# Sums of squares of q in a gated DeltaNet layer: block turns, row sums and one 0/1 product in place of eight one-column products

## The chip, the cores and the metric

The kernel runs on one core of a Trainium2 chip. The metric is device time in microseconds (us) of that core; the time of a kernel is the median of several executions. Five engines matter here: TensorE (PE in the profile; its weight loads are shown apart as PEld), VectorE (DVE), ScalarE (ACT), GpSimd (POOL) and SyncE (SP), which here only starts transfers.

## The reference

One decoder layer on 256 tokens of width 2048, all in float32. Cut to what matters:

```python
h = rmsnorm(x, norm_mix_w)
proj = h @ w_in                       # q, k, v, z, b, a, p_in, g_a, g_b
q, k, v = split(silu(causal_dwconv([q, k, v], conv_qkv_w)))
q = l2norm(q.reshape(1, 256, 16, 128)) * 128 ** -0.5   # per token and head
k = l2norm(k.reshape(1, 256, 16, 128))
o = gated_delta_rule(q, k, v, g_log, beta)   # chunks; a triangular solve in each
o = rmsnorm(o, gdn_norm_w) * silu(z)
mixed = sigmoid(g_a) * o + sigmoid(g_b) * pool_mixer(p_in)
x = x + mixed @ w_out
x = x + (gelu(causal_dwconv(gate)) * up) @ w_down   # gate, up = rmsnorm(x) @ w_up
y = rmsnorm(x, norm_final_w)
```

`l2norm` divides by the root of the sum of squares over the 128 dimensions of a head. A row of `o` is linear in its row of `q`, and `o` goes through an RMS norm, so the kernel doesn't normalise q at all: the sum of squares of q only enters the epsilon term of that norm. It needs one such sum for every token and head: 256 tokens by 4 heads in each of four groups of heads.

## The kernel before, in words

**Weights.** All weights stream from memory in tiles of 256 x 512 float32 (half a MB), in the order in which they are used. `weights()` (L102) hands out the next tile and starts the preparation of the tile two further on: SyncE loads it to `raw` (L112), ScalarE makes a rounded copy `whi` (L121), VectorE the rest `wlo = raw - whi` (L128). `whi` and `wlo` have three buffers each, so the copy for a tile can start once PE is through with the tile three places ahead of it.

**Products.** `gemm_a` (L147) multiplies the 256 tokens by 512 columns of weights: for each tile 4 times three products of 128 x 128 by 512 columns (L158 high by high, L159 low by high, L160 high by low), accumulated in a PSUM tile `psm`. After each half of a tile it calls `side()` (L134), which advances a generator by one `yield`: this is how the small work of the token mixer is written into the stream of large products.

**The loop over groups.** `for g in range(4)` (L779) handles four heads: projections k, q, v, then the pooling mixer, z and the gate, each a `gemm_a` over 8 tiles. After k and q their convolution and SiLU (`conv_silu`, L555) leave `kq` [128 dimensions, 4 heads, k or q, 256 tokens]. Then the generator `gdn` (L575) becomes the side work. In its order:

- decays `dec0`, `dec1` and Gram products k·k and k·q (L620, L622), scaled into `ga0`, `ga1` on DVE (L635, L639); the diagonals of k·k give the sums of squares of k (L625)
- the diagonal 32 x 32 blocks go to memory and come back spread over the partitions as `lb` (L653, L656)
- 31 steps of forward substitution on DVE (L665, L667) that read `lb` and write `tb`; `tb` goes to memory and comes back as blocks of `TTa` (L672, L675)
- four block turns `Ta <- TTa` on DVE (L686), then small products that complete the inverse (L699, L709, L719, L727) and apply it (L734, L739, L744; `w1`, `w2` are copied by ScalarE, L735 and L745)
- the outputs `po` (L752, L754, L755); the squares of q in place (L749, ScalarE); the sums of squares of q, `pn` (L760); squares of `po` on ScalarE and their sums on DVE (L765, L766); `ro` from both (L768, L769), a power on POOL (L770), the scaled output `on` (L772, L775).

`gated()` (L838) finishes the generator and multiplies `on` by the gates (L840, L841); `mixed()` turns the result (L203) for the output projection. After the fourth group eight tiles of the output projection that don't need it are multiplied first (L864).

`lb` and `on` share one buffer with `dec0` (tag "dec0", one buffer): each waits until the one before has been read.

**The order of the work.** Source order isn't engine order. Outside the first stage (`manual_schedule`, L288) the framework's planner orders the instructions of each engine by what its own model finds ready, with source order as priority. Each engine then runs its list strictly in that order and waits on semaphores. In the profile the squares of q (L749) start at 116.5 us in the first group, while the output products beside which they stand in the source (L752) start at 220.3 us.

A float32 product is shown as two MATMULs, each with a weight load of its own. The eight products of L760 in a group are 16 records; the loaded operand is 128 x 128 of squared q, the streamed one a single column of ones:

```python
pn = pg([P, 2, 4])
for t in range(2):
    for h in range(4):
        mm(pn[:, t, h : h + 1], q2[:, h, t * P : (t + 1) * P], ones[:, 0:1], start=True, stop=True)
```

Of the kernel before, what the change touches and what calls it, by code (L numbers as in the profile page):

```python
# [7 lines left out]
F32 = mybir.dt.float32  # L8
F32R = mybir.dt.float32r
I32 = mybir.dt.int32  # L10
AF = mybir.ActivationFunctionType
ALU = mybir.AluOpType

P = 128
S = 256
# [5 lines left out]
EPS = 1e-6  # L21
# [8 lines left out]
WAIT = 5  # L30
# [3 lines left out]
def kernel(  # L34
# [20 lines left out]
    nc = tc.nc  # L55
    mm = nc.tensor.matmul
# [10 lines left out]
    def nm(s):  # L67
        cnt[0] += 1
        return f"{s}_{cnt[0]}"

    def pg(shape=(P, 512)):
        return psg.tile(list(shape), F32, tag="g", name=nm("psg"))
# [135 lines left out]
    ones = cpool.tile([P, P], F32, name="ones")  # L208
    nc.gpsimd.memset(ones, 1.0)
    ident = cpool.tile([P, P], F32, name="ident")  # L210
# [19 lines left out]
    mp = mix.__enter__()  # L230
# [160 lines left out]
    for cq in range(4):  # L391
        pr = slice(32 * cq, 32 * cq + 32)
# [17 lines left out]
    nc.vector.tensor_tensor(id2, ident[:64, 0:32], ident[:64, 32:64], op=ALU.add)  # L410


    pba = pg([P, 2, S])
    for c in range(2):
        hi, lo = weights()
# [59 lines left out]
    for g, win in enumerate(WINDOWS):  # L475
# [3 lines left out]
        for cs in (slice(0, P + PAD), slice(P + PAD, NB)):  # L479
            b = bd[:, cs]  # L480
# [94 lines left out]
    def gdn(g, kq, vt, conv, res):  # L575
# [6 lines left out]
        dec0 = mp.tile([P, 4, S], F32, tag="dec0", name=nm("dec0"))  # L582
# [31 lines left out]
        for hp in range(2):  # L614
# [3 lines left out]
            for h in (h0, h0 + 1):  # L618
# [5 lines left out]
                for t, src in ((0, pg0[:, 0:P]), (1, pg1[:, 0, :])):  # L624
                    nc.vector.tensor_tensor_reduce(jk, src, ident, scale=1.0, scalar=0.0, op0=ALU.mult,  # L625
                                                   op1=ALU.add, accum_out=ssk[:, t, h : h + 1])
# [6 lines left out]
            for h in (h0, h0 + 1):  # L633
# [4 lines left out]
                                               op0=ALU.mult, op1=ALU.mult)  # L638
# [3 lines left out]
                                               op0=ALU.mult, op1=ALU.mult)  # L642
# [12 lines left out]
        for cq in range(4):  # L655
            nc.sync.dma_start(lb[32 * cq : 32 * cq + 32], cdd.rearrange("q (r j) i -> (q r) j i", j=B0))  # L656
        yield
        for _ in range(WAIT):
            yield
        tb = mp.tile([P, 8, B0], F32, tag="tb", name=nm("tb"))  # L660
# [18 lines left out]
        for h in range(4):  # L679
            for t in range(2):  # L680
                nc.scalar.activation(vt[:, t, h, :], vt[:, t, h, :], AF.Copy, scale=nk[:, t, h : h + 1])
        for _ in range(WAIT - 3):
            yield
        for r in range(NR):
            rs = slice(B0 * r, B0 * (r + 1))
            nc.vector.transpose(Ta[rs, :, rs], TTa[rs, :, rs])  # L686
# [50 lines left out]
        pr = pg([P, 4, P])  # L737
# [6 lines left out]
            mm(pw[:, h, :], TT[h // 2][:, 1, h % 2, :], vt[:, 1, h, :], start=True, stop=True)  # L744
        nc.scalar.copy(w2, pw)  # L745
        yield

        q2 = kq[:, :, 1, :]
        nc.scalar.activation(q2, q2, AF.Square)  # L749
        po = [pg([P, 4, P]) for t in range(2)]  # L750
        for h in range(4):
            mm(po[0][:, h, :], ga0[:, h, 256:384], w1[:, h, :], start=True, stop=True)  # L752
# [1 line left out]
            mm(po[1][:, h, :], ga0[:, h, 384:512], w1[:, h, :], start=True, stop=False)  # L754
            mm(po[1][:, h, :], ga1[:, h, P : 2 * P], w2[:, h, :], start=False, stop=True)  # L755
        yield
        pn = pg([P, 2, 4])
        for t in range(2):
            for h in range(4):
                mm(pn[:, t, h : h + 1], q2[:, h, t * P : (t + 1) * P], ones[:, 0:1], start=True, stop=True)  # L760
        ro = mp.tile([P, 2, 4], F32, tag="ro", name=nm("ro"))
        so = mp.tile([P, 2, 4], F32, tag="so", name=nm("so"))
        for t in range(2):
# [1 line left out]
            nc.scalar.activation(o2, po[t], AF.Square, scale=float(P) ** -0.5)  # L765
            nc.vector.tensor_reduce(so[:, t, :], o2, axis=mybir.AxisListType.X, op=ALU.add)  # L766
        yield
        nc.vector.tensor_scalar(ro, pn, EPS * P, EPS * EPS * P, op0=ALU.mult, op1=ALU.add)  # L768
        nc.vector.tensor_tensor(ro, ro, so, op=ALU.add)  # L769
        nc.gpsimd.tensor_tensor(ro, ro, epsx[:, 0:1].unsqueeze(2).to_broadcast([P, 2, 4]), op=ALU.pow)  # L770
        for t in range(2):
# [7 lines left out]
    for g in range(4):  # L779
        kq = mp.tile([P, 4, 2, S], F32, tag="kq", bufs=1, name=nm("kq"))  # L780
# [6 lines left out]
        vt2 = vt.rearrange("p t h d -> p t (h d)")  # L787
        res = []
        later.append(lambda g=g, kq=kq, vt=vt, res=res: side_work.__setitem__(0, gdn(g, kq, vt, v_conv(g, vt), res)))
        v_taps(g)  # L790
        e = evict(gemm_a(xh, xl, KD), rsh)
# [84 lines left out]
    for c in range(4):  # L876
# [9 lines left out]
        for k2 in range(2):  # L886
# [5 lines left out]
            for kk in range(2):  # L892
# [4 lines left out]
                                               op0=ALU.mult, op1=ALU.subtract)  # L897
# [59 lines left out]
    for t in range(2):  # L957
# [14 lines left out]
        for c in (0, 2, 1, 3):  # L972
            xs = xt[:, t, c * 512 : (c + 1) * 512]
            if c < 2:
                nc.vector.scalar_tensor_tensor(xs, xs, rs, nfin[:, c * 512 : (c + 1) * 512],
                                               op0=ALU.mult, op1=ALU.mult)
# [34 lines left out]
```

## Time and profile before

| | |
|---|---|
| median of 3 runs | 1581.47 us (1581.29 to 1581.65) |
| profiled execution | 1581.2 us, span 1579.4 us, mean granted TensorE clock 0.998 |
| busy | PE 1565.1 us, DVE 1066.2 us, ACT 745.4 us, POOL 45.0 us |
| read from memory | 297.56 MB |

The span runs from the first to the last instruction; the 1.8 us by which the profiled execution is longer lie around it. A row of a timeline gives start, length, engine, line, operation, output <- inputs, and in square brackets how long the engine stood idle before the row and what ended that. A row of the chain of waits gives start, length and what ran then on the chain that ended last. A row of groups gives the line, the operation, shapes and count, then busy time and the mean of one, then idle time before. A row of waits gives who waited for whom: us in total, times, the longest.

### The profile page before, as it was taken

The numbers are of one execution on the slowest core, as the hardware profiler recorded it, in microseconds if no ns is written. First come the engines' busy times: TensorE is split into PE (matmuls) and PEld (weight loads), VectorE is DVE, ScalarE is ACT, GpSimd is POOL, SyncE is SP. The second block draws the span as 40 slices with busy tenths as digits, with TensorE's granted clock in tenths as the row PEclk, the third lists the DMA queues.
The fourth block names the chain that finished last, engine by engine and source line by source line (L and its number), as shares of the span: only waits on it lengthen the run. The fifth ranks groups of instructions, "written<-read, shape, count | busy, mean of one in ns | idle before, by whom it ended". The sixth has DMA issues, their size and how long they took to land.

```text
span 1579.4 us, 21330 instructions
## 1 busy us (share of the span) xinstructions
PE 1565.1 (99%) x8086; PEld 1315.5 (83%) x8086; DVE 1066.2 (68%) x1619; ACT 745.4 (47%) x954; POOL 45.0 (3%) x69
## 2 busy tenths in 40 slices
PE   9999999999999999999999999999999999999997
PEld 8878888888878888788788888888888888888885
DVE  6897758885798657785556667766666667444445
ACT  6454445544555445544454544444444444434344
POOL 3010000000000000000000000000000000000000
PEclk9999999999999999999999999999999999999999
DMA  8776657675667647775656666666666666666663
GB/s 261 207 233 187 185 160 209 206 213 170 180 210 205 199 137 208 218 199 169 197 181 183 188 188 188 191 191 189 186 188 188 188 190 214 195 196 191 196 189 132
DMA packets 167925, 304.22 MB, mean 193 GB/s; under 512 B 19187, under 2 KB 22275, under 8 KB 167695
## 3 DMA queue, kind: packets, MB, share of 16 engines
q1 hardware_dynamic: 165088, 298.36, 64.1%
q10 hardware_dynamic: 2734, 4.51, 0.9%
q8 instruction: 63, 1.03, 0.3%
q14 instruction: 40, 0.32, 0.1%
HBM read 297.56 MB, written 5.27 MB: 192 GB/s over the span
## 4 chain that ended last, share of the span: by engine, by line
PE 96%; DVE 1%; DMA 1%; issue 1%; ACT 0%; DVEq 0%; POOLq 0%; POOL 0%; SPq 0%
PE psm L160 14%; PE psm L159 14%; PE psm L158 14%; PE psm L182 10%; PE psg L182 10%; PE psg L183 5%; PE psm L183 5%; PE psg L945 3%; PE psg L946 3%; PE psg L947 3%; PE psm L945 2%; PE psm L947 2%; PE psm L946 2%; PE psm L285 1%; PE psg L620 1%
## 5 line engine op out<-in xcount | busy, mean ns | idle before, releaser
L128 DVE TENSOR_TENSOR wlo<-raw,whi 128x1024 fp32r<-128x1024 f32 x528 | 645.1, 1223 | 421.0 <-ACT whi L121 412.1
L121 ACT CAST whi<-raw 128x1024 fp32r<-128x1024 f32 x530 | 557.6, 1053 | 737.9 <-PE psm L159 308.4
L160 PE MATMUL psm<-wlo,xhl 128*128 128x512 f32 x864 | 339.5, 393 | 0.7 <-DVE wlo L128 0.7
L158 PE MATMUL psm<-whi,xhl 128*128 128x512 f32 x864 | 339.0, 392 | 0.0
L159 PE MATMUL psm<-whi,xhl 128*128 128x512 f32 x864 | 338.4, 392 | 0.0
L182 PE MATMUL psm<-fhl,whi 128*128 128x512 f32 x704 | 246.2, 396 | 0.0
L182 PE MATMUL psg<-fhl,whi 128*128 128x512 f32 x704 | 238.0, 394 | 0.0
L183 PE MATMUL psm<-fhl,wlo 128*128 128x256 f32 x704 | 194.4, 279 | 0.0
L160 PEld LDWEIGHTS psm<-wlo,xhl 128*128 128x128 f32 x864 | 162.3, 188 | 34.3 <-DVE wlo L128 1.4
L159 PEld LDWEIGHTS psm<-whi,xhl 128*128 128x128 f32 x864 | 162.2, 188 | 33.4
L158 PEld LDWEIGHTS psm<-whi,xhl 128*128 128x128 f32 x864 | 162.3, 188 | 32.9 <-issue 0.2
L183 PE MATMUL psg<-fhl,wlo 128*128 128x256 f32 x704 | 178.7, 279 | 0.0
L182 PEld LDWEIGHTS psm<-fhl,whi 128*128 128x128 f32 x704 | 131.4, 188 | 30.5
L182 PEld LDWEIGHTS psg<-fhl,whi 128*128 128x128 f32 x704 | 129.2, 188 | 24.2
L183 PEld LDWEIGHTS psg<-fhl,wlo 128*128 128x128 f32 x704 | 132.5, 188 | 6.9
L183 PEld LDWEIGHTS psm<-fhl,wlo 128*128 128x128 f32 x704 | 132.5, 188 | 1.1
L945 PE MATMUL psg<-whi,hhi 128*128 128x512 f32 x176 | 68.6, 390 | 0.0
L945 PE MATMUL psm<-whi,hhi 128*128 128x512 f32 x176 | 68.5, 389 | 0.0
L946 PE MATMUL psm<-whi,hlo 128*128 128x512 f32 x176 | 68.5, 389 | 0.0
L946 PE MATMUL psg<-whi,hlo 128*128 128x512 f32 x176 | 68.5, 389 | 0.0
L947 PE MATMUL psm<-wlo,hhi 128*128 128x512 f32 x176 | 68.5, 389 | 0.0
L947 PE MATMUL psg<-wlo,hhi 128*128 128x512 f32 x176 | 61.7, 389 | 0.0
(241 smaller groups left out, 1489.7 us busy)
## 6 DMA issues: line engine op xcount, KB each, us to landing
raw<-in_w_in_dram SPq DMA_DIRECT2D x226, 512.0 KB, 4.3
raw<-in_w_up_dram SPq DMA_DIRECT2D x176, 512.0 KB, 4.5
raw<-in_w_down_dram SPq DMA_DIRECT2D x88, 512.0 KB, 4.4
raw<-in_w_out_dram SPq DMA_DIRECT2D x32, 512.0 KB, 3.9
mv<-vrow SPq DMA_DIRECT2D x12, 512.0 KB, 5.1
taps<-in_conv_qkv_w_dram SPq DMA_DIRECT2D x16, 256.0 KB, 6.0
raw<-in_pool_w_dram SPq DMA_DIRECT2D x8, 512.0 KB, 6.0
x<-in_x_dram SPq DMA_DIRECT2D x4, 512.0 KB, 8.2
```

What stands on the lines that cost most here:

```text
L121: nc.scalar.copy(hi, raw)
L128: nc.vector.tensor_tensor(lo, raw, hi.bitcast(F32), op=ALU.subtract)
L158: mm(ps[:, t, :], lh(k, t), hi[:, kk, :], start=(k == 0), stop=False)
L159: mm(ps[:, t, :], ll(k, t), hi[:, kk, :], start=False, stop=False)
L160: mm(ps[:, t, :], lh(k, t), lo[:, kk, :], start=False, stop=(k == nk - 1))
L182: mm(ps[f], hi[:, kk, fs], rhl(k), start=(k == 0), stop=False, skip_group_check=True)
L183: mm(ps[f][:, 1, :], lo[:, kk, fs], rhl(k)[:, 0, :], start=False, stop=(k == nk - 1), skip_group_check=True)
L285: mm(ps_k0[:, t, :], part(k, t), w[:, kk, :], start=(k == 0 and w is hi and part is xh), stop=(k == KD - 1 and w is lo))
L620: mm(pg0, kq[:, h, 0, 0:P], kq[:, h, :, :], start=True, stop=True)
L945: mm(acc[c][t], lh(k, t), hi[:, kk, :], start=(k == 0), stop=False)
L946: mm(acc[c][t], ll(k, t), hi[:, kk, :], start=False, stop=False)
L947: mm(acc[c][t], lh(k, t), lo[:, kk, :], start=False, stop=(k == KF - 1))
```

## The change

Once, in the preparation, a 0/1 matrix `sel` [128, 4, 32] is made on DVE: `sel[p, c, i]` is 1 where p mod 32 is i. In each group:

- the squares of q stand right behind the transfers of `lb` in the source
- behind the scaling of v, in place of two empty `yield`s, DVE turns every 32 x 32 block of the squares (`qx`, 128 x 1024, in the "dec0" buffer) and adds up runs of 32 (`qp`, 128 x 32): what is left is one partial sum for each quarter of the dimensions
- one product of `sel` with `qp` adds the quarters; it puts the sums of all tokens and heads into every quarter of the partitions, 32 columns wide
- `ro` takes for each quarter of the partitions the columns that belong to its tokens: four small DVE instructions in place of one

```diff
@@ preparation
+    sel = mp.tile([P, 4, 32], F32, name="sel")
+    nc.vector.tensor_reduce(sel[:, 0, :], ident.rearrange("p (b i) -> p i b", b=4), axis=mybir.AxisListType.X,
+                            op=ALU.add)
+    nc.vector.tensor_copy(sel[:, 1:4, :], sel[:, 0:1, :].to_broadcast([P, 3, 32]))
@@ gdn, behind the transfers of lb
         yield
+
+        q2 = kq[:, :, 1, :]
+        nc.scalar.activation(q2, q2, AF.Square)
         for _ in range(WAIT):
             yield
@@ gdn, behind the scaling of v, ahead of the block turns L686
-        for _ in range(WAIT - 3):
-            yield
+        qx = mp.tile([P, 4, S], F32, tag="dec0", name=nm("qx"))
+        nc.vector.transpose(qx, q2)
+        yield
+        qp = mp.tile([P, 32], F32, tag="qp", name=nm("qp"))
+        nc.vector.tensor_reduce(qp, qx.rearrange("p h (c j) -> p (h c) j", j=32), axis=mybir.AxisListType.X,
+                                op=ALU.add)
+        yield
@@ gdn, the outputs
-        q2 = kq[:, :, 1, :]
-        nc.scalar.activation(q2, q2, AF.Square)
@@
-        pn = pg([P, 2, 4])
-        for t in range(2):
-            for h in range(4):
-                mm(pn[:, t, h : h + 1], q2[:, h, t * P : (t + 1) * P], ones[:, 0:1], start=True, stop=True)
+        pn = pg([P, 4, 2, 4])
+        mm(pn.rearrange("p h t c -> p (h t c)"), sel.rearrange("p b i -> p (b i)"), qp, start=True, stop=True)
@@
-        nc.vector.tensor_scalar(ro, pn, EPS * P, EPS * EPS * P, op0=ALU.mult, op1=ALU.add)
+        for c in range(4):
+            pr = slice(32 * c, 32 * c + 32)
+            nc.vector.tensor_scalar(ro[pr], pn[pr, :, :, c].rearrange("p h t -> p t h"), EPS * P, EPS * EPS * P,
+                                    op0=ALU.mult, op1=ALU.add)
```

## The prediction

> **What bounds the kernel now.** I read the page first: busy shares, the 40 slices and the chain that ended last.
>
> ```profile
> PE 1565.1 (99%) x8086; PEld 1315.5 (83%) x8086; DVE 1066.2 (68%) x1619; ACT 745.4 (47%) x954; POOL 45.0 (3%) x69
> ...
> PE   9999999999999999999999999999999999999997
> ...
> DVE  6897758885798657785556667766666667444445
> ...
> PE 96%; DVE 1%; DMA 1%; issue 1%; ACT 0%; DVEq 0%; POOLq 0%; POOL 0%; SPq 0%
> ```
>
> PE is busy in every slice and makes 96% of the chain. The four groups lie in the first half, where DVE reaches 8 and 9 tenths, so DVE is the engine to fear. A busy PE could still hide waits, so next the waits of PE, for the whole span:
>
> ```profile
> PE psm L160 <- DVE wlo L128: 1.5, 3, 0.7
> PE psm L222 <- POOL ones L209: 1.0, 1, 1.0
> PE psm L158 <- ACT whi L121: 0.9, 1, 0.9
> ```
>
> That is 2.4 us of waiting for weights in the whole kernel. Inside the groups the time is the number of PE instructions by their spacing: PE time that goes is gained, and added DVE time costs only where PE comes to wait for it.
>
> **What is removed.** The chain gives spacing, without the overlap that is in a MATMUL's own duration:
>
> ```profile
> 43.90 1.01 PE psg L424 x8
> ...
> 189.54 0.62 PE psg L709 x32
> ...
> 220.42 0.89 PE psg L752 x8
> 221.54 1.68 PE psg L760 x16
> 223.22 0.34 PE psm L160
> 225.12 0.23 PE psm L158
> ...
> 754.96 1.68 PE psg L760 x16
> ```
>
> The one-column products take 1.68 us a group in the first group as in the last: 16 records of 105 ns. A 128-column product with the same 128 x 128 load takes 0.89/8 = 111 ns, so the load, not the column, sets the pace. The group rows say the same:
>
> ```profile
> L760 PEld LDWEIGHTS psg<-ones,kq 128*128 128x128 f32 x64 | 7.5, 192 | 0.0
> L754 PEld LDWEIGHTS psg<-w,ga 128*128 128x128 f32 x32 | 4.9, 192 | 0.0
> ```
>
> The new product is one pair with 32 streamed columns. The trace has no such pair on 128 rows; the nearest is L424 (64 rows, 32 columns) at 1.01/8 = 126 ns, so I take 2 x 0.126 = 0.25 us. From below the smallest products, L709 at 0.62/32 = 19 ns, would make it 0.04 us; from above, two whole MATMUL durations of L424:
>
> ```profile
> L424 PE MATMUL psg<-id,bat 64*128 64x32 f32 x8 | 1.1, 275 | 0.0
> ```
>
> that is 0.55 us. Saved per group: 1.68 - 0.25 = 1.43 us (1.13 to 1.64), in four groups **5.7 us** (4.5 to 6.6). Between L760 and L755 one large product stands alone in the first group (223.22, 0.34 us, against 0.23 us for one among its like at 225.12): going from small to large products costs about 0.1 to 0.2 us. If the planner makes one such passage more or less in each group, that is up to 0.8 us either way; I take none.
>
> [...]
>
> **What is added on DVE.** The rows nearest to the new instructions:
>
> ```profile
> L766 DVE TENSOR_REDUCE so<-o 128x4 f32<-128x512 f32 x8 | 5.5, 685 | 14.3 <-ACT o L765 14.3
> L547 DVE TENSOR_TENSOR vt<-vt,mv 128x1024 f32<-128x1024 f32 x12 | 14.6, 1218 | 0.0
> L686 DVE STREAM_TRANSPOSE T<-TT 32x256 f32<-32x256 f32 x16 | 7.0, 436 | 3.7 <-DMA TT<-tbd 3.3
> L712 DVE STREAM_TRANSPOSE TT<-T 32x128 f32<-32x128 f32 x16 | 4.9, 303 | 0.5
> ...
> L768 DVE TENSOR_SCALAR ro<-psg x4: 166/167/167, 223.3 to 756.7; 128x8 f32<-128x8 f32 x4
> ```
>
> Turn: (436 - 303)/128 = 1.04 ns a column plus 170 ns, so 1.23 us for 1024 columns, if 128 partitions cost no more than 32; four quarters one after another would be 4.9 us. Sum: 512 columns take as long as other instructions of that width, 1024 then 1.22 us. Four `ro` pieces in place of one: 3 x 0.167 = 0.5 us. Together 2.95 us a group. `sel` is two instructions of some 0.3 us once, which need only `ident`; like the `id2` made from it they can run in the first microseconds, ahead of the first weights.
>
> Where do turn and sum go? They need the squares and the "dec0" buffer, whose last reader is the end of the substitution (L665). What follows there, in the tightest group:
>
> ```profile
> 345.23 0.18 DVE L667 TENSOR_TENSOR tb<-tb,tmp 128x8 f32<-128x8 f32 x1
> 346.18 1.22 DVE L128 TENSOR_TENSOR wlo<-raw,whi 128x1024 fp32r<-128x1024 f32 x1 [0.77 <-ACT whi L121]
> 347.33 1.22 DVE L832 SCALAR_TENSOR_TENSOR sz<-gate,psm 128x1024 f32<-128x1024 f32 x1
> 349.38 0.29 DVE L662 COPY tb<-idb 128x256 f32<-128x256 f32 x1 [0.83 <-DMA tbd<-tb]
> 349.59 1.22 DVE L128 TENSOR_TENSOR wlo<-raw,whi 128x1024 fp32r<-128x1024 f32 x1
> 351.75 1.84 DVE L686 STREAM_TRANSPOSE T<-TT 32x256 f32<-32x256 f32 x4 [0.94 <-DMA TT<-tbd]
> ```
>
> DVE stands idle 0.77 + 0.83 + 0.94 = 2.5 us here while the inverse blocks go to memory and back, and 2.45 us of turn and sum fit: the rows between move back by at most 2.45 us, and the block turns still start when their data lands. Over all groups the two waits for these transfers alone are
>
> ```profile
> DVE tb L662 <- DMA tbd<-tb: 6.0, 3, 2.6
> ...
> DVE T L686 <- DMA TT<-tbd: 3.3, 4, 1.1
> ```
>
> 9.3 us against 9.8 us of new work. So I cost turn and sum at nothing; if that cover is gone, they land on `wlo` and on the block turns. How late may `wlo` be? The copies of two tiles in a row, and the first one's `wlo`:
>
> ```profile
> 172.21 1.05 ACT L121 CAST whi<-raw 128x1024 fp32r<-128x1024 f32 x1 [1.67 <-PE psm L159]
> 174.93 1.05 ACT L121 CAST whi<-raw 128x1024 fp32r<-128x1024 f32 x1 [1.67 <-PE psm L159]
> ```
>
> ```profile
> 173.30 1.22 DVE L128 TENSOR_TENSOR wlo<-raw,whi 128x1024 fp32r<-128x1024 f32 x1 [0.56 <-ACT whi L121]
> ```
>
> Each copy starts when PE leaves a tile, every 2.72 us. The tile copied at 172.21 is used two tiles later, from about 177.7, and its first `wlo` product is the third, near 178.1; its `wlo` is done at 174.52. The lead is 3.6 us, more than turn and sum together.
>
> **What is moved.** The squares (L749) issue nothing else; their row shows the planner already runs them 100 us ahead of the sums:
>
> ```profile
> L749 ACT ACTIVATE kq<-kq x4: 1064/1064/1066, 116.5 to 640.6; 128x1024 f32<-128x1024 f32 x4
> ```
>
> So the edit leaves them in place: nothing, covered by an ACT 47% busy; if that cover went, 1.06 us of ACT ahead of a `whi`, within the same lead. No transfer is moved. **New waits:** the turn waits on ACT's squares, done 50 us before; the product waits for `qp`, done some 45 us before it, with L755 and large products queued behind it; the `ro` pieces wait for the product, with `wlo` behind them. All are satisfied early. The `ro` pieces fall here, in the last group, whose outputs the output projection needs:
>
> ```profile
> 756.68 0.17 DVE L768 TENSOR_SCALAR ro<-psg 128x8 f32<-128x8 f32 x1 [0.59 <-PE psg L760]
> 757.02 1.23 DVE L128 TENSOR_TENSOR wlo<-raw,whi 128x1024 fp32r<-128x1024 f32 x1 [0.17 <-PE psm L160]
> 759.21 0.69 DVE L766 TENSOR_REDUCE so<-o 128x4 f32<-128x512 f32 x1 [0.96 <-ACT o L765]
> ```
>
> 0.59 + 0.17 + 0.96 us idle cover the 0.5 us; without cover it is 0.5 us, once. The outputs L755 come 1.43 us sooner behind the shorter product, so the chain of this tail and PE's filler move together, and PE's waits for weights stay as they are.
>
> **Sum.** 1581.2 us (span 1579.4 and 1.8 around it) - 5.7 = 1575.5 in the profiled execution; the median is 0.27 us above it, so **1575.8 us**, its own range 1574.0 to 1577.8 (6.6 + 0.8 to 4.5 - 0.8 gained).
>
> **The rivals.**
>
> *Turn or sum ends up between the landing of the inverse blocks and their turns.* Then the products behind are late, and PE, in order, waits. Its lead there:
>
> ```profile
> 355.41 0.31 PE L699 MATMUL psg<-T,ga 32*32 32x32 f32 x4
> ...
> 716.63 0.31 PE L699 MATMUL psg<-T,ga 32*32 32x32 f32 x4
> ```
>
> ```profile
> 715.56 0.44 DVE L686 STREAM_TRANSPOSE T<-TT 32x256 f32<-32x256 f32 x1
> ```
>
> 0.6 us in the last group (716.00 to 716.63), 1.8 us in the second (351.75 + 1.84 to 355.41). Both in front cost 2.45 less the lead: 1.85 us in the last, 0.65 in the second, between these in the others, some 4 us; only one in front 0.6 us. Middle 2.4, so 1578.2, at worst 1579.9. For: the planner's model needn't know these durations. Against: the two are ready right after the loop, before any landing.
>
> *The removed products cost the path little*, because PE's weight loads run ahead: at the 19 ns of L709, 4 x 14 x 0.019 = 1.1 us, so 1580.4. [...] Against: 105 ns in the chain rows.
>
> *Slower: the turn runs quarter by quarter.* At 4.9 us, turn and sum need 24.5 us in four groups; 9.3 us of holes and leads of some 1.5 us a group (between 0.6 and 1.8) cover 15.3; the other 9.2 us are PE waits ahead of L699, so 1581.5 - 5.7 + 9.2 = 1585.0. It decides from a turn of 4.0 us (gain gone), and from 4.8 us it is slower. For: no row turns more than 32 partitions. Against: every other DVE row costs by columns, 128 partitions or fewer. [...]
>
> *The last group's waits go as well* (another order in its tail): up to 2.4 us more, 1573.4.
>
> **How the numbers follow.** Forecast 0.64, the delayed block turns 0.16, cheap products 0.06, slow turn 0.09, waits gone 0.05. Forecast and first rival hold 0.80: 1574.0 to 1579.9. Within 0.2% (3.2 us, about what a measurement can tell from no change) is 1578.3 and above: faster is 0.64 + 0.05 + over half of the first rival = 0.78, same 0.13, slower 0.09.
>
> **What would show it.** In the profile after: L760 gone and its successor with 8 MATMULs in all, some 0.25 us a group on the chain; a turn and a sum of about 1.2 us each between the last L667 and L686; PE's waits still some 2 to 4 us in all. A turn above 4 us, new waits of L699 or of L160, or a chain that leaves PE inside a group would prove me wrong.

## The result, and the profile after

The changed kernel takes **1578.47 us** in the median of 21 runs (1576.01 to 1580.38), the kernel before 1581.42 us beside it (1581.1 to 1582.61): a ratio of 0.9981, with a 95% interval of 0.9974 to 0.9987. It is faster by 2.95 us (0.19%); 5.7 were forecast, and 1578.47 lies above the forecast's own range of 1574.0 to 1577.8. The profiled execution took 1578.94 us, its span 1577.2. From its page, the busy times; and its waits of PE for weights:

```profile
PE 1560.4 (99%) x8030; PEld 1309.2 (83%) x8030; DVE 1076.8 (68%) x1641; ACT 745.2 (47%) x954; POOL 45.2 (3%) x69
```

```profile
PE psm L160 <- DVE wlo L128: 3.0, 4, 1.4
...
PE psm L158 <- ACT whi L121: 0.9, 1, 0.9
```

PE has 56 records less, 14 in each group, and DVE 10.6 us more work. But PE waits 3.0 us for `wlo` where it waited 1.5, and the longest wait is 1.4 us where it was 0.7. (In the changed kernel L759, L764, L766, L767, L770 are the old L744, L752, L754, L755, L760; L674 is the old L665, L662 the old L656.)

**Where along the span is the gain?** The large products are the same in both kernels, so the start of the n-th product L158 can be compared. Timelines of PE, before and after, the products 200, 330, 408, 560, 800 and 1000 (counted from 0):

```profile
187.11 0.39 PE L158 MATMUL psm<-whi,xhl 128*128 128x512 f32 x1
...
295.62 0.39 PE L158 MATMUL psm<-whi,xhl 128*128 128x512 f32 x1
...
350.56 0.39 PE L158 MATMUL psm<-whi,xhl 128*128 128x512 f32 x1
...
475.30 0.39 PE L158 MATMUL psm<-whi,xhl 128*128 128x512 f32 x1
...
662.96 0.39 PE L158 MATMUL psm<-whi,xhl 128*128 128x512 f32 x1
...
818.48 0.39 PE L158 MATMUL psm<-whi,mhi 128*128 128x512 f32 x1
```

```profile
187.53 0.39 PE L158 MATMUL psm<-whi,xhl 128*128 128x512 f32 x1
...
294.71 0.39 PE L158 MATMUL psm<-whi,xhl 128*128 128x512 f32 x1
...
350.59 0.39 PE L158 MATMUL psm<-whi,xhl 128*128 128x512 f32 x1
...
473.80 0.39 PE L158 MATMUL psm<-whi,xhl 128*128 128x512 f32 x1
...
659.52 0.39 PE L158 MATMUL psm<-whi,xhl 128*128 128x512 f32 x1
...
816.30 0.39 PE L158 MATMUL psm<-whi,mhi 128*128 128x512 f32 x1
```

The distance is +0.42, -0.91, +0.03, -1.50, -3.44 and -2.18 us. Read as steps: the start loses 0.42; the small products of the first group gain 1.33; something early in the second group takes 0.94 back; its own small products gain 1.53, the third group's 1.94; and in the last group, where 1.43 were to be gained, 1.26 are lost. The sum, 2.2 us, is the difference of the spans.

**The last group's tail.** PE before, then after:

```profile
764.93 0.50 PE L158 MATMUL psm<-whi,mhi 128*128 128x512 f32 x1 [0.91 <-ACT whi L121]
...
766.18 0.50 PE L160 MATMUL psm<-wlo,mhi 128*128 128x512 f32 x1 [0.52 <-DVE wlo L128]
...
770.92 0.50 PE L160 MATMUL psm<-wlo,mhi 128*128 128x512 f32 x1 [0.28 <-DVE wlo L128]
```

```profile
763.13 0.50 PE L158 MATMUL psm<-whi,mhi 128*128 128x512 f32 x1 [0.91 <-ACT whi L121]
...
765.29 0.79 PE L160 MATMUL psm<-wlo,mhi 128*128 128x512 f32 x1 [1.43 <-DVE wlo L128]
765.88 0.63 PE L158 MATMUL psm<-whi,mhi 128*128 128x512 f32 x1
766.31 0.63 PE L159 MATMUL psm<-whi,mlo 128*128 128x512 f32 x1
...
771.54 0.51 PE L160 MATMUL psm<-wlo,mhi 128*128 128x512 f32 x1 [0.27 <-DVE wlo L128]
```

The three waits grow from 1.71 to 2.61 us, and behind the long one the products are 0.43 us apart instead of 0.23, up to 768.45. The view by windows shows what that is (after; its columns are stretch, length, PE busy, records, granted clock, DMA share and GB/s):

```profile
core 0: us, PE busy (x), PEclk, DMA share, GB/s
...
765.00:769.00 4.00, 3.71 (x10) 0.57 0.40 131
```

The same stretch before:

```profile
765.00:769.00 4.00, 3.48 (x15) 1.00 0.67 215
```

The granted clock was 0.57 in these 4 us; before, behind waits of 0.91 and 0.52, it was 1.00. From 765.29 to 768.45 are seven steps in 3.16 us, and the seven from 766.18 to 767.90 took 1.72 before, so the clock costs some 1.4 us and the waits 0.9. That is 2.3 us of the 2.7 between what was to be gained and what was lost.

**Why the tail is thin.** The outputs L767, which the result of the group needs, were to come 1.43 us sooner. Small products of the last group, before and after, and the copy of `w2` for which L767 has to wait:

```profile
752.79 1.05 PE L744 MATMUL psg<-vt,TT 128*128 128x128 f32 x8
...
756.82 0.38 PE L755 MATMUL psg<-w,ga 128*128 128x128 f32 x2
```

```profile
753.28 1.05 PE L759 MATMUL psg<-vt,TT 128*128 128x128 f32 x8
...
755.28 0.31 PE L770 MATMUL psg<-qp,sel 128*128 128x32 f32 x2
755.42 0.48 PE L159 MATMUL psm<-whi,mlo 128*128 128x512 f32 x1
...
757.33 0.38 PE L767 MATMUL psg<-w,ga 128*128 128x128 f32 x2
```

```profile
754.37 0.59 ACT L760 COPY w<-psg 128x512 f32<-128x512 f32 x1 [0.97 <-PE psg L759]
```

From the first product with `w2` to L755 it was 4.03 us; to L767 it is 4.05. The removed time is filled with eight large products (755.42 to 757.33), though the copy was done at 754.96. In the first three groups the order puts 14 or 15 there: 5.65, 5.64 and 5.41 us where it was 4.03, 3.72 and 3.71. PE waits for nothing there, but the group's result is later, and the large products spent here no longer stand behind it. Counted in large products from the start, L755 stood at 2760 in the last group, L767 stands at 2784. The first product with `w2` also moved, from 2759 to 2776: turn and sum stand on DVE ahead of the block turns (the experiments below show that this is what moves it).

**The second group** meets its block transfer. DVE before; then DVE and PE after:

```profile
307.06 0.42 DVE L665 TENSOR_TENSOR tmp<-lb,tb 128x248 f32<-128x248 f32 x1 [3.52 <-DMA lb<-cdd]
```

```profile
311.23 0.42 DVE L674 TENSOR_TENSOR tmp<-lb,tb 128x248 f32<-128x248 f32 x1 [5.53 <-DMA lb<-cdd]
311.56 1.22 DVE L128 TENSOR_TENSOR wlo<-raw,whi 128x1024 fp32r<-128x1024 f32 x1
```

```profile
312.83 0.50 PE L160 MATMUL psm<-wlo,xhl 128*128 128x512 f32 x1 [0.64 <-DVE wlo L128]
```

DVE stands at the first step of the substitution until `lb` has landed; a `wlo` is queued behind it, and PE comes to wait for that one. Here the second pair of Gram products stands at large product 986; before, it was at 930.

### The profile page after: what moved, and what is told of

Its sections match the earlier page's. It is cut to its first block, busy times and chain, and to the rows that moved or that the text cites. A ratio compares the mean times of both kernels' runs of the same rounds, so it can differ in the third digit from the quotient of the medians.

```text
span 1577.2 us, 21251 instructions
## 1 busy us (share of the span) xinstructions
PE 1560.4 (99%) x8030; PEld 1309.2 (83%) x8030; DVE 1076.8 (68%) x1641; ACT 745.2 (47%) x954; POOL 45.2 (3%) x69
## 4 chain that ended last, share of the span: by engine, by line
PE 96%; DVE 1%; DMA 1%; issue 1%; ACT 0%; POOL 0%; DVEq 0%; POOLq 0%; SPq 0%
PE psm L160 14%; PE psm L159 14%; PE psm L158 14%; PE psm L182 10%; PE psg L182 10%; PE psg L183 5%; PE psm L183 5%; PE psg L958 3%; PE psg L959 3%; PE psg L960 3%; PE psm L958 2%; PE psm L960 2%; PE psm L959 2%; PE psm L285 1%; PE psg L626 1%
## 5 line engine op out<-in xcount | busy, mean ns | idle before, releaser
L160 PE MATMUL psm<-wlo,xhl 128*128 128x512 f32 x864 | 340.0, 394 | 1.3 <-DVE wlo L128 1.3
L158 PE MATMUL psm<-whi,xhl 128*128 128x512 f32 x864 | 339.2, 393 | 0.0
L160 PEld LDWEIGHTS psm<-wlo,xhl 128*128 128x128 f32 x864 | 162.2, 188 | 35.6 <-DVE wlo L128 2.8
L158 PEld LDWEIGHTS psm<-whi,xhl 128*128 128x128 f32 x864 | 162.3, 188 | 32.7 <-ACT ev L521 0.2
```

What stands on the lines that cost most here:

```text
L158: mm(ps[:, t, :], lh(k, t), hi[:, kk, :], start=(k == 0), stop=False)
L160: mm(ps[:, t, :], lh(k, t), lo[:, kk, :], start=False, stop=(k == nk - 1))
```

## The experiments

**Theory:** the sizes were right (the saving is there wherever the order stays clean), and what is missing is the order: the emptied place was filled with more large products than it held time for, and turn and sum push the last group's chain back, so cover runs out in the tail. (Filler means the large products that PE can run while a group's small steps wait for each other; cover is the filler that is left behind a step. A position is the number of large products that start ahead of a step.) **Rivals:** the added DVE work costs the rest (A), or the saving itself is smaller than it looks (B). Each kernel ran beside the kernel before, which had medians of 1581.4 to 1581.9 us. In the table "gain" is the difference of the medians (5 to 21 runs each); the ratio is that of all runs, not of the medians, and its intervals are 2 to 4 us wide, so kernels that lie within a us or two of each other are told apart by their traces, not by their medians. The other columns are steps as above, from one profiled execution each, plus for gained; `lb` is the step from product 330 to 408, early in the second group; "last" is the last group, in the kernels with a reserve without the 2.95 us that the reserve gains alone. The column of the first group ends at product 330; in the rows marked * it holds some 0.9 us of another stall (below).

| kernel | median, us | ratio, interval | gain | first group | `lb` | last |
|---|---|---|---|---|---|---|
| changed kernel | 1578.47 | 0.9981 [0.9974, 0.9987] | 2.95 | 1.33 | -0.94 | -1.26 |
| old way in the last group | 1578.8 | 0.9984 [0.9975, 0.9993] | 2.7 | 1.37 | -1.29 | 0.06 |
| both ways | 1582.14 | 1.0004 [0.9995, 1.0012] | -0.6 | 0.0 | 0.0 | -0.65 |
| turn, sum, eight products last | 1578.38 | 0.9983 [0.9974, 0.9991] | 3.2 | 1.48 | -1.18 | -0.65 |
| one product alone last | 1577.45 | 0.9972 [0.9960, 0.9983] | 4.15 | 0.51* | -1.82 | 0.89 |
| turn and sum behind | 1577.7 | 0.9973 [0.9962, 0.9985] | 3.9 | 0.38* | -0.98 | 0.89 |
| outputs first | 1577.35 | 0.9971 [0.9961, 0.9982] | 4.5 | 1.57 | -1.18 | 0.79 |
| outputs first, turn behind | 1577.51 | 0.9970 [0.9959, 0.9982] | 4.4 | 1.57 | -0.89 | 1.58 |
| before, with reserve | 1578.85 | 0.9983 [0.9975, 0.9992] | 2.7 | 0.0 | 0.0 | 0 |
| changed, reserve | 1574.75 | 0.9959 [0.9946, 0.9971] | 6.8 | 1.48 | -0.78 | -0.29 |
| turn behind, reserve | 1575.89 | 0.9965 [0.9952, 0.9977] | 5.7 | 0.41* | -0.52 | -0.14 |
| outputs first, reserve | 1575.76 | 0.9963 [0.9950, 0.9975] | 6.1 | 1.57 | -1.33 | -0.21 |
| all three | 1574.24 | 0.9950 [0.9937, 0.9962] | 7.6 | 1.57 | -0.57 | 1.57 |

### Is it the saving, the DVE work or the tail?

The old way in the last group only (there without turn and sum, and with the one `ro` instruction), the change in the first three:

```diff
+        if g < 3:
             pn = pg([P, 4, 2, 4])
             mm(pn.rearrange("p h t c -> p (h t c)"), sel.rearrange("p b i -> p (b i)"), qp, start=True, stop=True)
+        else:
+            pn = pg([P, 2, 4])
+            for t in range(2):
+                for h in range(4):
+                    mm(pn[:, t, h : h + 1], q2[:, h, t * P : (t + 1) * P], ones[:, 0:1], start=True, stop=True)
```

> The change in the first three groups only; the last group keeps the eight one-column products and the single ro instruction. Theory (the saving is 1.4 us a group, but in the last group the shorter product lets the planner spend large products of the output projection's reserve ahead of L755, so PE runs dry in the tail, waits and drops its clock): three savings stay, 4.3 us, and the tail waits are as before, some 1.7 us without a drop of the clock; about 1577.5 us, not slower than the full change at 1578.5. Rival A (the added DVE work costs PE some 0.7 us in each group) and rival B (the removed products were worth only 0.7 us a group): three quarters of the gain of 2.9 us, 1579.2 us.

1578.8: between the two numbers, and nearer to that of the rivals. The trace decides: the first three groups gain 1.37, 1.53 and 1.21 us, not 0.7, the tail has the waits of before again (0.91, 0.53, 0.28 us, with products 0.23 us apart behind them), and the last group neither gains nor loses; what the theory had left out is the 1.29 us lost at `lb`. So the last group's part of the change is worth nothing as it stands: 0.25 us by the two gains (2.95 and 2.7), a loss of 1.3 us by the two profiles (-1.26 and 0.06).

Turn and sum added in all groups (their result unused), the eight products and the one `ro` instruction kept; shown against the changed kernel:

```diff
-        pn = pg([P, 4, 2, 4])
-        mm(pn.rearrange("p h t c -> p (h t c)"), sel.rearrange("p b i -> p (b i)"), qp, start=True, stop=True)
+        pn = pg([P, 2, 4])
+        for t in range(2):
+            for h in range(4):
+                mm(pn[:, t, h : h + 1], q2[:, h, t * P : (t + 1) * P], ones[:, 0:1], start=True, stop=True)
```

> Turn and sum on DVE are kept, but nothing reads the sums; the eight one-column products a group and the single ro instruction are back. It is the price of the added DVE work by itself (2.45 us a group). Theory: no price but where an order happens to put a wait in front of a wlo, 1581.4 to 1582.3 us. Rival A: 0.7 us a group on top of before, 1584.2 us. Rival B: 1581.4 us.

1582.14; the interval includes no change at all. Turn and sum in four groups cost at most 1.9 us by that interval, in the profile 0.65 in the last group, where the outputs now stand at 2776 in place of 2760. By itself the DVE work (rival A, 1584.2) doesn't carry the missing 2.7 us.

A reserve of six and six weight tiles of the output projection in place of six and two, put into the changed kernel and into the one before:

```diff
-    early = [gemm_a(at(mhi), at(mlo), KD, range(n)) for n in (6, 2)]
+    early = [gemm_a(at(mhi), at(mlo), KD, range(n)) for n in (6, 6)]
```

> The changed kernel with 12 tiles of the output projection in reserve for the tail of the last group instead of 8 (six of the first column block, six of the second; the loads follow in the same order). Theory: PE's waits of 2.6 us in the tail and the half clock behind them (1.3 us) go: 1578.5 - 3.9 = 1574.6 us, and no row of the tail shows products 0.43 us apart. Rivals A and B: only the waits that were there before the change go, 1.7 us, 1576.8 us.

> The kernel before with the same larger reserve. All theories: the waits of its tail go, 1.7 us, 1579.7 us. What tells them apart is the distance to the changed kernel with the same reserve: theory 4.8 to 5.7 us, rivals A and B 2.9 us.

1574.75 and 1578.85: 4.1 us apart where the plain kernels are 2.95 apart. By the medians more cover brings part of the missing gain back, but the intervals are too wide to tell 4.1 from 2.95; what speaks against rival B is the step of the first group: 1.33 to 1.57 us in every kernel that has the one product there and no other wait of PE. The kernel before gained 2.7 us by its reserve where 1.7 were expected: more than the waits that went, and why isn't shown. What is left stands in the tail of the changed kernel with the reserve:

```profile
770.11 1.03 PE L203 MATMUL psg<-ident,sz 128*128 128x128 f32 x8
771.66 0.73 PE L158 MATMUL psm<-whi,mhi 128*128 128x512 f32 x2 [0.52 <-ACT mhi L866]
773.04 0.50 PE L159 MATMUL psm<-whi,mlo 128*128 128x512 f32 x1 [0.64 <-DVE mlo L867]
```

Now PE waits for the result itself: behind its turn (L203) there is no large product left that doesn't need it, and ScalarE's and DVE's halves of it are waited for in full. The kernel before with the reserve has no wait there.

### Which part pushes the last group's chain back?

Turn and sum with the eight products kept, in the last group only; and the other way round, one product without turn and sum (the diff). The second of these leaves the sums of q out of the last group's result: its product reads other columns.

```diff
+        if g < 3:
             qx = mp.tile([P, 4, S], F32, tag="dec0", name=nm("qx"))
             nc.vector.transpose(qx, q2)
...
-        mm(pn.rearrange("p h t c -> p (h t c)"), sel.rearrange("p b i -> p (b i)"), qp, start=True, stop=True)
+        qs = qp if g < 3 else q2[:, 0, 0:32]
+        mm(pn.rearrange("p h t c -> p (h t c)"), sel.rearrange("p b i -> p (b i)"), qs, start=True, stop=True)
```

> The first three groups have the change; the last group does the turn and the sum on DVE (their result unused) and keeps the eight products. Theory (the order of PE is laid out again, and in the last group the turn and the sum push the chain back by some 17 large products of 0.216 us): the tail keeps the longer PE waits of the changed kernel (the two waits at the weights together over 1.5 us, with products at half rate behind them), 1580 to 1581, 1 to 2 us over the kernel that has the old way in the last group (1578.8). Rival (only the missing filler of eight products sets the tail): the tail as before the change, waits of 0.9 and 0.5 us, 1578.8.

> In the last group the one product reads 32 columns of the squares themselves, and the turn and the sum are left out, so the sums of q are left out of the result there. Theory (turn and sum push the chain by some 17 large products, the missing products by some 15 again): with the one left, about a third of the tail's loss of 2.7 us comes back: 1577.2 to 1578.1, the longest PE wait of the tail under 1.43 us. Rival 1 (turn and sum alone make the loss): all of it comes back, 1575.8. Rival 2 (the missing filler alone makes it): as the changed kernel, 1578.5.

(The large products of these kernels start 0.23 us apart, not 0.216.) The first measured 1578.38, not 1580 to 1581: the size was wrong. The long wait is not there, the waits are 0.91, 0.53 and, new, 0.91 in place of 0.28 us, and the last group loses 0.65:

```profile
761.57 0.50 PE L158 MATMUL psm<-whi,mhi 128*128 128x512 f32 x1 [0.91 <-ACT whi L121]
...
762.83 0.50 PE L160 MATMUL psm<-wlo,mhi 128*128 128x512 f32 x1 [0.53 <-DVE wlo L128]
...
766.30 0.50 PE L158 MATMUL psm<-whi,mhi 128*128 128x512 f32 x1 [0.91 <-ACT whi L121]
```

The second measured 1577.45, inside the range given, though six runs from 1575.37 to 1578.79 would allow either rival; its trace has the same three waits, and the last group keeps 0.89 of the 1.58 us. So either shift alone (outputs at 2776 or 2774 in place of 2760) costs about 0.7 us, and both together (2784) cost 2.8 (1.58 to -1.26), the long wait and the low clock with it. The loss isn't a sum of two parts: some 15 large products cost a fourth of what 24 cost.

Turn and sum issued behind the block turns, in all groups, without and with the reserve:

```diff
             bt = nc.vector.transpose(Ta[rs, :, rs], TTa[rs, :, rs])
         yield
+        with tc.issue_after(bt.ins):
+            qx = mp.tile([P, 4, S], F32, tag="dec0", name=nm("qx"))
+            nc.vector.transpose(qx, q2)
```

> All groups have the change, but the turn and the sum are issued on DVE behind the block turns of the chain. Theory (turn and sum ahead of the block turns hold the chain up): in the last group the two levels of block steps come back to their place of before and only the missing filler shifts the end, so the tail is that of the kernel without turn and sum in its last group: 1577.0 to 1578.2. Rival 1: the sum now comes late for the one product and PE waits for it, 1579 or more. Rival 2 (the place on DVE is of no account): 1578.5.

> The turn and the sum behind the block turns, and a reserve of six weight tiles for each of the two first column blocks of the output in place of six and two. Theory (the tail's loss is cover that ran out): with the reserve and the earlier chain the waits of the tail go, and the last group's 1.43 us is kept: 1573.5, in 1573.0 to 1574.3. Rival (the last group's saving is lost to something else than the chain's place): as with the reserve alone, 1574.75.

1577.7, inside the range given (its interval alone would allow 1578.5 too), with the tail of the last experiment. But 1575.89 with the reserve, above the range: no better than the reserve alone, and with the same two waits of 0.52 and 0.64 us. My theory that the chain's place alone decides fell here; in this kernel w2 stands at 2759 as before, yet the outputs at 2774.

### The filler held back

The large products that the order puts between the new product and the outputs are issued behind the outputs; nothing else in the source is touched. The numbers in the diff are positions: from each of the four on, up to 30 large products are held until the last of the outputs:

```diff
+    def behind():
+        g = next((g for g, n in enumerate((720, 1385, 2081, 2777)) if n <= nth[0] < n + 30), None)
+        nth[0] += 1
+        return tc.issue_after(held[g]) if g in held else nullcontext()
...
+                    with behind():
                         mm(ps[:, t, :], lh(k, t), hi[:, kk, :], start=(k == 0), stop=False)
...
-            mm(po[1][:, h, :], ga1[:, h, P : 2 * P], w2[:, h, :], start=False, stop=True)
+            last = mm(po[1][:, h, :], ga1[:, h, P : 2 * P], w2[:, h, :], start=False, stop=True)
+        held[g] = last.ins
```

> The changed kernel, with the large products that its order puts between the new product and the second half of the outputs (7 to 15 in each group) held back behind these outputs. Nothing else in the source is changed; in the order the Gram products of the second group also come back to large product 930. Theory (the emptied place was filled with more large products than the eight one-column products cost, so the group's result came later, the second group met its block transfer, and the tail ran out of cover): the stall of the second group (0.64 us and what follows) goes, the tail loses some 0.7 us in place of 2.7, all four savings stay: 1576.3, in 1575.5 to 1577.0. Rival 1 (the place of these products is of no account): 1578.5. Rival 2 (PE now waits at the outputs for the copy of w2): waits of about 0.5 us a group, 1578 or more.

1577.35, above the range given. From the first product with `w2` to the outputs it is now 2.47 us in every group, without a wait of PE (rival 2 falls), and the first group gains 1.57. The last group keeps 0.79 instead of losing 1.26. But the stall of the second group didn't go, though the Gram products are back at 930: that part of the theory was wrong (below).

> As the one before, with the turn and the sum on DVE behind the block turns. Theory: the tail has the order of before (w2 at large product 2759, outputs at 2760) and keeps the last group's saving too: 1575.6, in 1574.8 to 1576.3, which is what was forecast for the change itself. Rival (turn and sum in front cost nothing in the tail): the same as the one before.

This was to be 1574.8 to 1576.3. The profiled execution took 1575.74 us, its span 1574.0; but the six times are 1575.43, 1575.74 and four from 1577.19 to 1578.0, so the median, 1577.51, misses the range and is no better than that of the kernel before it. What sets the two heights apart no trace here shows, and what follows holds for the lower one. In it the tail is that of before, wait for wait:

```profile
759.54 0.50 PE L166 MATMUL psm<-whi,mhi 128*128 128x512 f32 x1 [0.91 <-ACT whi L121]
...
760.81 0.50 PE L170 MATMUL psm<-wlo,mhi 128*128 128x512 f32 x1 [0.54 <-DVE wlo L128]
...
765.53 0.50 PE L170 MATMUL psm<-wlo,mhi 128*128 128x512 f32 x1 [0.28 <-DVE wlo L128]
```

(L166, L168 and L170 are L158 to L160 here.) All four groups keep their saving: 1.57, 1.60, 1.92 and 1.58 us.

> The outputs first, as in the first of these, with the reserve of six and six weight tiles. Theory (in the kernel with the reserve alone, 1574.75, the waits of 0.52 and 0.64 us for the group's own result were cover spent ahead of the outputs): these waits go or fall under 0.3 us, the stall of the second group goes: 1573.3, in 1572.7 to 1574.2. Rival (the result's chain is too long for the cover whatever the order): the waits stay, 1574.3 to 1574.9.

1575.76, above both ranges, and the waits of 0.52 and 0.64 stayed: the rival's signature. With the reserve, turn and sum in front alone use up the cover again.

> Outputs first, turn and sum behind the block turns, reserve of six and six. Theory: 5.7 us from the change and 2.7 us from the reserve add up: 1573.0, in 1572.5 to 1573.9, no wait over 0.3 us in the tail. Rival (something else still holds the last group's result): 1574.75 as with the reserve alone.

**1574.24**, the lowest median of all, though above the range given and not clear of the 1574.75 of the reserve alone: 7.6 us under the kernel before, of which the reserve gives that kernel 2.7 by itself. The waits of the tail are gone. All waits of PE in the span:

```profile
PE psm L170 <- DVE wlo L128: 1.1, 3, 0.7
PE psm L232 <- POOL ones L219: 1.0, 1, 1.0
PE psm L295 <- ACT whi L121: 0.5, 1, 0.5
PE psg L352 <- DMA cfrows<-in_conv_ffn_w_dram: 0.3, 1, 0.3
```

With the reserve, three kernels out of four lose the last group's saving (-0.29, -0.14, -0.21 us); only the one in which neither the filler nor turn and sum stand ahead of the outputs keeps it (1.57). Each of these figures is from one execution.

### The stall that stayed

In every kernel with the saving in its first group, the step with DVE's wait for `lb` in the second loses 0.5 to 1.8 us, 0.2 to 1.5 of it PE's wait for the `wlo` behind; with both ways, where PE is not early, it loses nothing. (In the rows marked * another `wlo` is late in that group, behind DVE's work on v, which waits for rows from memory: with turn and sum behind, PE waits 0.76 us for it at 283.78.) SyncE's queue before, and in the kernel with outputs first and turn behind (start and length of issue):

```profile
298.47 1.85 SPq L112 DMA_DIRECT2D raw<-in_w_in_dram  x2
300.69 1.74 SPq L656 DMA_DIRECT2D lb<-cdd  x4
```

```profile
297.88 0.90 SPq L112 DMA_DIRECT2D raw<-in_w_in_dram  x2
299.01 1.74 SPq L672 DMA_DIRECT2D lb<-cdd  x4
```

```profile
307.21 0.42 DVE L684 TENSOR_TENSOR tmp<-lb,tb 128x248 f32<-128x248 f32 x1 [4.87 <-DMA lb<-cdd]
```

`lb` is issued 1.68 us sooner and is there 0.15 us later (307.21 against 307.06), while PE is 1.20 us ahead. PE came earlier, the transfer didn't. My guess is that the two weight loads right ahead of it hold it up. In five profiles with the Gram products at 930, the step that needs `lb` starts 8.6 to 9.3 us after the first of these loads is issued, whether `lb` itself is issued 1.1 us after that load (outputs first, the same with turn behind, all three) or 2.2 and 2.5 us (the kernel before, and the one with both ways). But no run took the loads away; it stays open.

## Why the prediction was right, and where it wasn't

- **The number.** The forecast was 1575.8 in 1574.0 to 1577.8, and 1578.47 lies above it, with about half of the gain. It lies in the wider 1574.0 to 1579.9 only by the price of the first rival, the delayed block turns, and those weren't delayed (below): that the time falls inside is luck. By the prediction's own line of 0.2%, 1578.3, it falls under "same", to which it gave 0.13 (the 21 runs do tell it from no change). Its sign of being wrong came, too: a new wait of L160, 0.64 us in the second group, and one of 1.43 us in the tail. And that rival's price was added up wrong: in the profile before, the lead in the third group is 0.25 us (the last block turn ends at 535.97, L699 starts at 536.22), not between 0.6 and 1.8, so with both in front it would have cost some 5.5 us and not 4.
- **Removed products.** Right. The new pair costs 0.14 us up to the next product (755.28 to 755.42), I took 0.25; the group saves 1.57 us where the order is clean. The 105 ns of the chain rows were the price, not the 19 ns of L709, from which the rival of the cheap products was worked out. With filler in between the first group saves 1.33 to 1.48 (four profiles): one more passage between small and large products, 0.1 to 0.24 us, for which I had allowed 0.2 at most.
- **Added DVE work.** Right in size, and no quarter-by-quarter turn:

```profile
702.86 1.24 DVE L693 STREAM_TRANSPOSE qx<-kq 128x1024 f32<-128x1024 f32 x1
...
705.13 1.21 DVE L696 TENSOR_REDUCE qp<-qx 128x32 f32<-128x1024 f32 x1
...
711.44 0.43 DVE L701 STREAM_TRANSPOSE T<-TT 32x256 f32<-32x256 f32 x1 [2.84 <-DMA TT<-tbd]
```

  1.23 and 1.22 were forecast, and the rival of 4.9 us is out: the turn of 128 partitions took 1.24 us, and the rows of 32 partitions had given 1.23 for 1024 columns. Their place is where I put it, right behind the substitution, and the block turns still wait 2.84 us for their data (in the other groups 0.59, 2.17 and 1.13 us), so the rival of the delayed block turns is out too. But they still move the last group's chain by 17 large products in the order of PE, worth 0.65 us there alone (seen in the kernel with both ways and in the one with turn, sum and eight products last).
- **The step that failed:** "The outputs L755 come 1.43 us sooner behind the shorter product, so the chain of this tail and PE's filler move together, and PE's waits for weights stay as they are." They came no sooner (4.05 us after the first product with `w2` against 4.03, and 24 large products later) and in the other groups later by 1.6 to 1.9 us. So PE's waits for weights in the tail grew by 0.9 us, with 1.4 us of low clock behind them. I took the removed time off PE's list and left the rest of the list alone; the list is made anew. Holding the filler back and putting turn and sum behind gave the tail of before, and the last group its 1.58 us, in the execution that was profiled (the median of that kernel didn't follow); with the reserve added it gave 1.57 us and the lowest median.
- **Not forecast:** `lb` in the second group, 0.94 us. I had counted PE's waits, and this was a wait of DVE with 3.5 us of idle time, with no `wlo` behind it in time; PE 1.2 us ahead was enough to make it one. In the changed kernel the second pair of Gram products also stands 56 large products later, but putting it back didn't remove the wait.
- **The start:** 0.42 us late in the profile; `sel` was put at nothing. The twelve kernels with `sel` are all late at product 200, by 0.17 to 0.89 us, but the one other kernel without it (before, with reserve) is 0.23 late too, so whether `sel` costs anything isn't shown.

The sum in the profile: three groups gave 1.33 + 1.53 + 1.94 = 4.8 us where 4.3 were forecast (why the third gives more than 1.57 isn't settled), the last took 1.26 in place of giving 1.43, `lb` took 0.94 and the start 0.42: 2.2 us, and 2.95 between the medians. The account holds for the profiled execution, 0.47 us above the median.

## What to carry to other kernels

Time taken out of an ordered engine's list was only gained at the end here where what fills the hole didn't push a late chain later (in the profiles the last group lost 1.26 us, and gained 1.58 with the filler held back and turn and sum behind): after an edit, compare the positions of the chain's small steps, counted in units of the filler, not only their durations. Where filler covers the wait for a chain at the end of a stage, look how much of it is left: here the loss came in jumps, about 0.7 us for some 15 large products and 2.8 for 24. And look at what is queued behind an engine's wait: DVE's 3.52 us for `lb` cost PE nothing before, and behind the 5.53 us after it PE waited 0.64 us for a `wlo`.

## What the runs showed of the hardware that was not expected

- After PE's waits of 0.91 and 1.43 us within 3.1 us, the granted clock was 0.57 over 765 to 769 us and products came at 0.43 instead of 0.23 us for about 2.6 us; behind waits of 0.91, 0.53 and 0.91 us (they end at 761.57, 762.83 and 766.30 in the kernel with turn, sum and eight products last) the products came 0.23 us apart again. A narrower window, 765.2 to 768.5, gives 0.50. In this execution 0.9 us more of waiting went with 1.4 us more for the clock.
- The changed kernel's times spread over 4.4 us (1576.01 to 1580.38, 21 runs), those of the kernel before over 1.5. Each run has its mean granted clock: of the changed kernel's runs, the 11 at 0.998 have a median of 1577.68 us, the 10 at 0.997 or less (the profiled one among them) 1579.06. Of the 27 runs of the kernel before that ran beside the first experiments, those at 0.998 and at 0.997 have 1581.55 and 1581.52. The 1.4 us between the first two fit the low clock of the tail, so about half of the runs may have had it; only single executions were profiled, so that isn't shown.
